# A hybrid Fourier / attention / DeltaNet block: the context triangular systems spread over all partitions, eight interleaved rows of a system in each

## The chip, the cores and the metric

The kernel runs on one core of a Trainium2 chip. The metric is the time of one execution on the device in microseconds (us); a version is judged by the median of its runs. Engines are named as in the profile: PE (TensorE matmul), PEld (TensorE weight load), DVE (VectorE), ACT (ScalarE), POOL (GpSimd) and SP (SyncE, which here only issues DMAs; its queue is SPq in the profile).

## The reference

One layer mixes 1024 latent tokens (width 1024) and 256 context tokens. One input projection feeds three groups of heads: a Fourier group, attention (8 query heads, 2 key/value heads) and a gated DeltaNet with 4 heads of 64. Then come an output projection and a squared-ReLU MLP. Cut to the DeltaNet, whose triangular systems the change touches:

```
z = h @ lp['w_in']                       # f, aq, ak, av, dqkv, dz, gates
dqkv = silu(dwconv(dqkv, conv_w))        # q, k, v of the DeltaNet
lmat = where(strict, einsum('nbhid,nbhjd->nbhij', kb, kc) * decay, 0.0)
tmat = triangular_solve(eye + lmat, eye, left_side=True, lower=True)
u = einsum('nbhij,nbhjd->nbhid', tmat, vb)
w = einsum('nbhij,nbhjd->nbhid', tmat, kb * exp(gc)[..., None])
# per chunk n: S -> S', o   (a sequential scan over the chunks)
o_f, s_f = chunk_gdn(forward);  o_b, s_b = chunk_gdn(reversed)
```

Each chunk of each head and of each direction has a unit triangular matrix that has to be inverted. The scan over the context gives the states from which the scan over the latents starts, so context and latents both need their inverses (tmat).

## The kernel before, in words

The kernel uses chunks of CK = 32 tokens: NCL = 32 latent chunks and NCC = 8 context chunks. With 4 heads and 2 directions d that makes 256 latent systems and 64 context systems, each 32x32. All products are emulated in three matmuls from a high and a low half (L236, L237, L238: high by high, high by low, low by high), so each weight is split: ACT writes the high half (helper L220) and DVE subtracts it (L448) for the low half. L238 is the matmul that needs the low half.

The stage in question lies about 200 to 320 us after the start. In it PE runs, one after the other, the second half of the query projection, the DeltaNet's v columns (`w_dv`), its q columns (`w_dq`), and the columns `w_dz` and `w_f` for the gate and the Fourier group, between them short groups of matmuls that regroup v by chunk (`compact`, L629) and at the end the transposes of the keys (`k_T`), with which attention begins. `conv_proj` clears the padding of the convolution's input with three memsets on POOL (L579 to L581), projects on PE and copies with ACT; `conv_silu` convolves and applies SiLU on DVE (L596, L597, L598, L603, L605). The regrouping L629 of the second v half waits for L603.

Beside that run the triangular systems. `grams()` forms the matrices L on PE, masks them on DVE (L739) and stores them to a DRAM scratch `lsc[d]` (L740). `solve(d, lat, eng)` (L747 to L764) then inverts: direction 0 on DVE, direction 1 on POOL, each first for the context and then for the latents. One system lies in one partition as a 32x32 matrix U: the 32 context systems of a direction take 32 partitions (in the half of `KQT` that q takes later, tile z2a in the profile), the 128 latent systems all 128 (in `trib[d]`, tile fbase). Four DMAs load (L754), a POOL memset puts ones on the diagonal (L755), 30 steps of two instructions each (L760 multiplies a column by a row into `tmps[d]`, L761 adds) do the elimination in place, and four DMAs store to the scratch `tsc[d]` (L764). L895 and L897 load the inverses, of the context and of the latents, into `TT`, which the scan reads.

The two solves are generators that `tick()` advances while PE instructions are being written (`systems()` for direction 0, `system1()` for direction 1); after w_dq they are forced on until both context solves are written, and at the end drained. A scheduler then fixes the order of instructions on each engine while the kernel is built. An engine works strictly in that order, and so does SP: what stands behind a waiting instruction waits too. PE's order and ACT's order are the same in both kernels.

Of the kernel before, what the change touches and what calls it, by code (L numbers as in the profile page):

```python
# [14 lines left out]
ALU = mybir.AluOpType  # L15
AX = mybir.AxisListType

P = 128
# [9 lines left out]
CK = 32  # L28
VC_ = 68
NCL = S // CK  # L30
NCC = CTX // CK
# [143 lines left out]
def view(b, off, *shape):  # L175
    v = Buf.__new__(Buf)
    v.arena, v.shape, v.at = b.arena, (P,) + shape, b.at + off
    v.n = int(np.prod(shape))
    return v
# [12 lines left out]
def body(tc, t, out):  # L192
# [3 lines left out]
    with ctx:  # L196
# [14 lines left out]
        V, G, T, Y, SC = nc.vector, nc.gpsimd, nc.tensor, nc.sync, nc.scalar  # L211

        def buf(*shape, top=False, a=None, at=None):
            return Buf(a or Fa, (P,) + shape, top, at)
# [338 lines left out]
        for p, xs in enumerate((xs1, xs2, xs3, xs4)):  # L553
            norm_in(xs)
            g, c0 = ((0, 256), (1, 0), (1, 256), (2, 0))[p]
# [18 lines left out]
        KQT, KTC, KC, VC = kqt(), ktc(), kc(), vc()  # L574
        zrb, yb, thb = buf(S + 2 + CTX + 2), buf(S + CTX), buf(S + CTX)
        trib = [buf(S) for _ in range(2)]
# [112 lines left out]
        for d in range(2):  # L689
            R = view(vc, 0, NCA, CK)() if d else FF_[1]  # L690
            mk = C[("mle", "mge")[d]]
            G.tensor_tensor(R, GTT[:, 2 + d, :].unsqueeze(2).to_broadcast([P, NCA, CK]), mk.unsqueeze(1).to_broadcast([P, NCA, CK]), op=ALU.mult)
            for c in range(0, NCA, 16):
                n = min(16, NCA - c)
# [25 lines left out]
        lsc = [dram.tile([P, NCA, CK], F32, name=f"lsc{d}") for d in range(2)]  # L720
        tsc = [dram.tile([P, NCA, CK], F32, name=f"tsc{d}") for d in range(2)]
# [5 lines left out]
        def grams():  # L727
            for c in list(range(NCL, NCA, 8)) + list(range(0, NCL, 8)):
                b = gb.next()
                bv = b[:, 0 : 8 * CK].rearrange("p (c w) -> p c w", w=CK)  # L730
                for q in range(8):
                    for h in range(4):
                        hp, h2 = h // 2, h % 2
                        r = slice(64 * h2, 64 * h2 + 64)
                        k_ = KQT[r, hp, 0, (c + q) * CK : (c + q + 1) * CK] if c < NCL else KTC[r, hp, (c + q - NCL) * CK : (c + q - NCL + 1) * CK]
                        pe(T.matmul(bv[32 * h : 32 * h + 32, q, :], k_, k_, start=True, stop=True))
                for d in range(2):
                    l_ = lst.next()()
                    V.scalar_tensor_tensor(l_, bv, -1.0, FF_[d][:, c : c + 8, :], op0=ALU.mult, op1=ALU.mult)  # L739
                    Y.dma_start(lsc[d][:, c : c + 8], l_)  # L740
                yield
                yield
            done.append(1)

        tmps = [buf(256) for _ in range(2)]

        def solve(d, lat, eng):  # L747
            c0, n = (0, NCL) if lat else (NCL, NCC)
            nu = 4 * n
            pr_ = slice(0, nu) if lat else slice(nu * d, nu * d + nu)  # L750
            flat = trib[d]()[pr_] if lat else KQT[pr_, 0, 1, :]
            U = flat.rearrange("p (m i) -> p m i", i=CK)
            for h in range(4):
                Y.dma_start(U[h * n : (h + 1) * n], lsc[d][32 * h : 32 * h + 32, c0 : c0 + n, :].rearrange("j c i -> c j i"))  # L754
            G.memset(flat[:, 0 : S : CK + 1], 1.0)  # L755
            for s in range(1, CK - 1):
                j, ms, is_ = (s, slice(0, s), slice(s + 1, CK)) if d == 0 else (CK - 1 - s, slice(CK - s, CK), slice(0, CK - 1 - s))
                nm, ni = s, CK - 1 - s
                tv = tmps[d]()[pr_, 0 : nm * ni].rearrange("p (m i) -> p m i", i=ni)
                eng.tensor_tensor(tv, U[:, ms, j : j + 1].to_broadcast([nu, nm, ni]), U[:, j : j + 1, is_].to_broadcast([nu, nm, ni]), op=ALU.mult)  # L760
                eng.tensor_tensor(U[:, ms, is_], U[:, ms, is_], tv, op=ALU.add)  # L761
                yield
            for h in range(4):
                Y.dma_start(tsc[d][32 * h : 32 * h + 32, c0 : c0 + n, :].rearrange("j c i -> c j i"), U[h * n : (h + 1) * n])  # L764

        def systems():
            for _ in range(GRAM):
                yield
            yield from grams()
            yield from solve(0, False, V)  # L770
            solved.append(1)
            yield from solve(0, True, V)

        def system1():
            while not done:
                yield
            yield from solve(1, False, G)
            solved.append(1)
            yield from solve(1, True, G)


        def q_sink(half):
# [10 lines left out]
        for half in range(2):  # L793
            w_q = wgroup([(COL_AQ + half * 256, 256)])
            if half:
                tasks += [[systems(), 2, 3], [system1(), 2, 3]]
                pinned = True
            proj_N(w_q, 256, range(NT), q_sink(half))
# [584 lines left out]
        for n in range(NPR * 5):  # L1383
            j, k = n // 5, n % 5
# [8 lines left out]
            h = j // 4  # L1393
# [114 lines left out]
        for n4 in range(4):  # L1508
# [9 lines left out]
            for q in range(NT):  # L1518
                b = omr.next()[:, 0:256]
                for k in (0, 1, 2, 3, 4, 6, 7, 5):  # L1520
                    h, l = halves[k // 4]
# [221 lines left out]
        for pn, (prods, blocks) in enumerate(PASSES):  # L1743
            for pc in range(NPC):
                U, W = {}, {}
# [3 lines left out]
                for w in blocks:  # L1749
                    W[w] = raww.next()()  # L1750
                    j, k = int(w[0]) - 1, int(w[1]) - 1
# [11 lines left out]
                for n in prods:  # L1763
                    if n in WSUM:
                        x, y, op = WSUM[n]
# [38 lines left out]
```

## Time and profile before

| | us |
|---|---|
| time, median of 3 runs (lowest to highest) | 1457.31 (1456.09 to 1457.76) |
| time of the profiled execution | 1456.26 |
| span of the profiled execution (first to last instruction) | 1454.5 |
| busy: PE / DVE / ACT / POOL | 1384.1 / 1005.7 / 703.6 / 668.5 |
| context solve on DVE, first to last instruction | 201.87 to 261.85 |
| latent solve on DVE | 261.89 to 313.81 |
| context solve on POOL | 207.24 to 267.00 |
| latent solve on POOL | 267.24 to 320.42 |

A row of a timeline gives the start in us from the beginning of the span, the duration in us, engine, line and operation, the tile written and the tiles read, their partitions x elements, and in brackets how long the engine had been idle before it and what released it. Short neighbouring instructions on DVE overlap by some 0.1 us in their records. The clock column (PEclk) of a table of windows is the TensorE clock that was granted, as a share of full speed.

### The profile page before, as it was taken

What the parts mean: (1) busy time and instruction counts of PE and PEld (TensorE: products, weight loads), DVE (VectorE), ACT (ScalarE), POOL (GpSimd) and SP (SyncE); (2) the same over time, 40 slices, a digit from 0 to 9 for tenths busy, and PEclk for the clock granted to TensorE, in tenths of its full rate; (3) what the DMA queues carried; (4) which work ended last, traced back from release to release, by engine and by line L of the source; (5) the groups of instructions that cost most, each with busy time, mean ns of one, the idle gap of its engine ahead of it and who ended that gap; (6) DMA issues with size and microseconds to landing.
All of it is one profiled execution on the core that took longest, in us unless ns stands there. A gap on an engine that the chain in (4) does not pass through costs nothing.

```text
span 1454.5 us, 28942 instructions
## 1 busy us (share of the span) xinstructions
PE 1384.1 (95%) x11462; PEld 1117.6 (77%) x11462; DVE 1005.7 (69%) x1695; ACT 703.6 (48%) x1239; POOL 668.5 (46%) x739
## 2 busy tenths in 40 slices
PE   4899988989999999989899899999999999999997
PEld 1677977766777777778799777888888888888886
DVE  0774679986878877786633887655556576776984
ACT  1742422323777777776412654554545443443331
POOL 2653679973446466374433733444443100010782
PEclk8999999999999999999999999999999999999999
DMA  8973141242000010042322315544446898766641
GB/s 316 334 257 125 45 118 44 53 93 76 9 10 24 9 38 4 17 142 80 95 84 91 106 55 183 168 147 134 141 151 217 307 392 269 245 230 215 197 157 58
DMA packets 137304, 197.67 MB, mean 136 GB/s; under 512 B 45021, under 2 KB 80463, under 8 KB 136911
## 3 DMA queue, kind: packets, MB, share of 16 engines
q1 hardware_dynamic: 136464, 195.12, 41.0%
q8 instruction: 90, 1.47, 0.4%
q10 hardware_dynamic: 703, 0.69, 0.2%
q14 instruction: 47, 0.39, 0.1%
HBM read 149.84 MB, written 45.94 MB: 135 GB/s over the span
## 4 chain that ended last, share of the span: by engine, by line
PE 47%; DVE 2%; POOL 2%; DMA 1%; issue 1%; ACT 1%; SPq 0%; DVEq 0%; POOLq 0%; ACTq 0%
PE bk L237 8%; PE bk L238 8%; PE bk L236 8%; PE ba L236 7%; PE ba L237 7%; PE ba L238 7%; PE bk L233 1%; DVE z1b L1335 0%; PE ba L233 0%; DMA fbase<-w_out 0%; POOL rbase L1470 0%; DMA fbase<-la 0%; DMA la<-fbase 0%; DVE rbase L998 0%; POOL z2c L1734 0%
## 5 line engine op out<-in xcount | busy, mean ns | idle before, releaser
L220 ACT ACTIVATE rbase<-fbase 128x512 fp32r<-128x512 f32 (+3 forms) x255 | 171.4, 685 | 87.5 <-PE bk L237 54.8
L220 ACT ACTIVATE fbase<-bk 128x512 f32<-128x512 f32 (+3 forms) x224 | 124.9, 561 | 150.8 <-PE bk L233 81.0
L233 PE MATMUL bk<-rbase 128*128 128x256 f32 (+2 forms) x984 | 173.3, 311 | 4.4 <-ACT fbase L220 2.6
L233 PEld LDWEIGHTS bk<-rbase 128*128 128x128 f32 (+1 forms) x984 | 132.3, 175 | 34.1 <-ACT fbase L220 3.4
L220 ACT ACTIVATE z1c<-fbase 128x512 fp32r<-128x512 f32 (+1 forms) x120 | 76.8, 653 | 138.5 <-DMA fbase<-w_ff 51.8
L233 PE MATMUL ba<-rbase 128*65 128x512 f32 (+4 forms) x576 | 138.4, 343 | 5.6 <-DVE rbase L998 4.8
L1503 POOL TENSOR_TENSOR fbase<-fbase 128x512 f32<-128x512 f32 x64 | 87.4, 1366 | 114.4 <-DVE z1c L1470 81.2
L220 ACT ACTIVATE fbase<-fbase 128x512 f32<-128x512 f32 (+4 forms) x148 | 95.9, 659 | 90.6 <-POOL fbase L1626 27.2
L1708 POOL TENSOR_TENSOR z2c<-z2c,fbase 128x512 f32<-128x512 f32 x16 | 31.1, 1969 | 203.8 <-ACT z2c L220 127.9
L974 DVE TENSOR_REDUCE fbase<-ba 128x1 f32<-128x512 f32 (+1 forms) x192 | 106.4, 593 | 19.6 <-PE ba L233 18.3
L220 ACT ACTIVATE rbase<-z1d 128x1024 fp32r<-128x1024 f32 x61 | 63.0, 1055 | 101.9 <-PE bk L237 81.8
L1470 DVE TENSOR_TENSOR z1c<-fbase,z1c 128x512 fp32r<-128x512 f32 x112 | 91.5, 820 | 23.6 <-ACT z1c L220 19.7
L1470 DVE TENSOR_TENSOR rbase<-z1d,rbase 128x1024 fp32r<-128x1024 f32 x61 | 84.9, 1407 | 31.1 <-ACT rbase L220 30.9
L998 POOL TENSOR_TENSOR rbase<-fbase,rbase 128x512 fp32r<-128x512 f32 x56 | 72.1, 1287 | 67.2 <-ACT rbase L220 63.0
L236 PE MATMUL bk<-rbase 128*128 128x512 f32 x256 | 99.7, 389 | 0.0
L237 PE MATMUL bk<-rbase 128*128 128x512 f32 x256 | 99.7, 389 | 0.0
L238 PE MATMUL bk<-rbase 128*128 128x512 f32 x256 | 99.6, 389 | 0.0
L998 DVE TENSOR_TENSOR rbase<-fbase,rbase 128x512 fp32r<-128x512 f32 x104 | 80.5, 774 | 25.7 <-ACT rbase L220 25.3
L1470 DVE TENSOR_TENSOR rbase<-fbase,rbase 128x1024 fp32r<-128x1024 f32 (+1 forms) x65 | 81.0, 1265 | 21.8 <-ACT rbase L220 21.6
L233 PEld LDWEIGHTS ba<-rbase 128*65 128x65 f32 (+1 forms) x576 | 76.2, 155 | 23.3 <-DVE rbase L998 5.9
L238 PE MATMUL ba<-rbase 128*128 128x512 f32 x192 | 74.8, 389 | 0.0
L237 PE MATMUL ba<-rbase 128*128 128x512 f32 x192 | 74.7, 389 | 0.0
(349 smaller groups left out, 3815.8 us busy)
## 6 DMA issues: line engine op xcount, KB each, us to landing
fbase<-w_ff SPq DMA_DIRECT2D x70, 512.0 KB
u<-fbase SPq DMA_DIRECT2D x112, 256.0 KB
z2a<-w_mod SPq DMA_DIRECT2D x36, 512.0 KB
z1d<-w_ff SPq DMA_DIRECT2D x34, 512.0 KB
z1d<-u SPq DMA_DIRECT2D x33, 512.0 KB
fbase<-u SPq DMA_DIRECT2D x23, 512.0 KB
fbase<-w_in SPq DMA_DIRECT2D x16, 512.0 KB
fbase<-x SPq DMA_DIRECT2D x14, 512.0 KB
```

The costliest lines, as they stand in the source:

```text
L220: return SC.activation(o, i, f, **k)
L233: pe(T.matmul(o, l, r, start=start, stop=stop))
L236: pe(T.matmul(o, lh, rh, start=start, stop=False))
L237: pe(T.matmul(o, lh, rl, start=False, stop=False))
L238: pe(T.matmul(o, ll, rh, start=False, stop=stop))
L974: V.tensor_reduce(st4[:, z : z + 1], b, AX.X, ALU.max)
L998: (G if k2 in GP and not any(a <= n < b for a, b in NGP) else V).tensor_tensor(hl[:, :, 1], p, f32(hl[:, :, 0]), op=ALU.subtract)
L1470: eng.tensor_tensor(lo, i, f32(hi), op=ALU.subtract)
L1503: G.tensor_tensor(w[nm], w[a], w[b], op=op)
L1708: G.tensor_tensor(c, c, G2[cs_.start // 512], op=ALU.mult)
```

## The change

`solve` is split into `solve_ctx` and `solve_lat`. The latent part is the old code. In the context part a system takes four partitions instead of one. Partition group g (32 partitions, 8 for each head) holds of every system the rows g, g+4, ..., 8 rows of 32, as R in `KQT[:, 0, 1, d*256 : d*256+256]` (tile z2a), and a whole copy N of the matrix L in `trib[d]` (tile fbase). R begins as the identity (a memset to 0 and four memsets to 1 on POOL, L754 and L756 of the changed kernel), and 31 steps of two instructions (L762, L763) subtract multiples of its columns, each on 128 partitions; a step takes only the rows that can be other than zero.

```diff
-        def solve(d, lat, eng):
-            flat = trib[d]()[pr_] if lat else KQT[pr_, 0, 1, :]
...
+        def solve_ctx(d, eng):
+            N = trib[d](None, (P, CK, CK))
+            flat = KQT[:, 0, 1, d * 8 * CK : (d + 1) * 8 * CK]
+            R = flat.rearrange("p (m i) -> p m i", i=CK)
+            for g in range(4):
+                for h in range(4):
+                    Y.dma_start(N[32 * g + NCC * h : 32 * g + NCC * (h + 1)], lsc[d][32 * h : 32 * h + 32, NCL:, :].rearrange("j c i -> c j i"))
+            G.memset(flat, 0.0)
+            for g in range(4):
+                G.memset(flat[32 * g : 32 * g + 32, g : 8 * CK : CK + 4], 1.0)
+            for s in range(CK - 1):
+                j = s if d == 0 else CK - 1 - s
+                rs, is_ = (slice(0, j // 4 + 1), slice(j + 1, CK)) if d == 0 else (slice(j // 4, 8), slice(0, j))
+                nm, ni = rs.stop - rs.start, CK - 1 - s
+                tv = tmps[d]()[:, 0 : nm * ni].rearrange("p (m i) -> p m i", i=ni)
+                eng.tensor_tensor(tv, R[:, rs, j : j + 1].to_broadcast([P, nm, ni]), N[:, j : j + 1, is_].to_broadcast([P, nm, ni]), op=ALU.mult)
+                eng.tensor_tensor(R[:, rs, is_], R[:, rs, is_], tv, op=ALU.add)
+                yield
+            for g in range(4):
+                for h in range(4):
+                    Y.dma_start(tsc[d][32 * h + g : 32 * h + 32 : 4, NCL:, :].rearrange("r c i -> c r i"), R[32 * g + NCC * h : 32 * g + NCC * (h + 1)])
+
+        def solve_lat(d, eng):
+            nu = 4 * NCL
+            flat = trib[d]()
...
-            yield from solve(0, False, V)
+            yield from solve_ctx(0, V)
             solved.append(1)
-            yield from solve(0, True, V)
+            yield from solve_lat(0, V)
```

Summed over the steps, a context solve had 60 instructions of 30 to 240 elements, 4960 elements per partition in all for each of the two operations; it has 62 of 8 to 76 elements now, 1560. The loads of a direction are 16 DMAs of 8 partitions instead of 4, with four times the bytes; the stores 16 instead of 4 with the same bytes. Because N lies in `trib[d]`, the latent loads into the same buffer stand behind the context solve now. Numbers of lines behind L747 shift; those that are used below: L774 (latent loads), L775 (the latent diagonal's memset), L780 and L781 (latent steps), L767 (context stores), L753 (context loads); L816, the scaling of v on POOL, is L836.

How the scheduler orders this now is shown at three places. On DVE, around the low halves (L448) of `w_dq`; L922, L923 and L913 are small copies for the projection's rows. Before:

```order
L760 TENSOR_TENSOR fbase<-z2a 32x184
L761 TENSOR_TENSOR z2a<-z2a,fbase 32x23x8
L922 CAST rbase<-fbase 128x10
L760 TENSOR_TENSOR fbase<-z2a 32x168
L923 TENSOR_SCALAR rbase<-fbase 128x10
L448 TENSOR_TENSOR z1a<-fbase,z1a 128x1024
L761 TENSOR_TENSOR z2a<-z2a,fbase 32x24x7
L913 TENSOR_SCALAR rbase<-fbase 128x136
L448 TENSOR_TENSOR z1a<-fbase,z1a 128x1024
```

In the changed kernel, at the same place:

```order
L763 TENSOR_TENSOR z2a<-z2a,fbase 128x7x7
L762 TENSOR_TENSOR fbase<-z2a,fbase 128x42
L942 CAST rbase<-fbase 128x10
L943 TENSOR_SCALAR rbase<-fbase 128x10
L763 TENSOR_TENSOR z2a<-z2a,fbase 128x7x6
L448 TENSOR_TENSOR z1a<-fbase,z1a 128x1024
L762 TENSOR_TENSOR fbase<-z2a,fbase 128x35
L933 TENSOR_SCALAR rbase<-fbase 128x136
L448 TENSOR_TENSOR z1a<-fbase,z1a 128x1024
```

L448 still stands inside the context solve, behind 47 of 60 solve instructions before and 52 of 62 now, none of more than 76 elements.

On POOL, where the context solve ends and the latent one begins. Before:

```order
L760 TENSOR_TENSOR fbase<-z2a 32x58
L761 TENSOR_TENSOR z2a<-z2a,fbase 32x29x2
L760 TENSOR_TENSOR fbase<-z2a 32x30
L761 TENSOR_TENSOR z2a<-z2a,fbase 32x30
L580 MEMSET fbase 128x2
L760 TENSOR_TENSOR fbase<-fbase 128x30
L761 TENSOR_TENSOR fbase<-fbase 128x30
L581 MEMSET fbase 128x1
```

In the changed kernel:

```order
L762 TENSOR_TENSOR fbase<-z2a,fbase 128x8
L763 TENSOR_TENSOR z2a<-z2a,fbase 128x8
L580 MEMSET fbase 128x2
L581 MEMSET fbase 128x1 x2
L775 MEMSET fbase 128x32
L836 TENSOR_TENSOR z2a<-z2a,fbase 128x2560
L579 MEMSET fbase 128x1
L580 MEMSET fbase 128x2
L775 MEMSET fbase 128x32
L780 TENSOR_TENSOR fbase<-fbase 128x30
```

The diagonal of DVE's latent systems (the first L775) now stands behind POOL's whole context solve, and the large L836 ahead of POOL's latent solve instead of in its midst.

On SP, from the context loads to the context inverses; `lsc_1451` and `tsc_1453` are direction 0 (DVE), `lsc_1452` and `tsc_1454` direction 1 (POOL), `qd` holds the queries, and the L444 are the halves of weights: one of `w_dq`, two of `w_dz`, two of `w_f`. Before:

```order
L754 DMA fbase<-lsc_1451 32x32x32 x2
L444 DMA fbase<-w_in 128x4x256
L786 DMA qd<-z2a 128x256
L754 DMA fbase<-lsc_1451 32x32x32 x2
L754 DMA fbase<-lsc_1452 32x32x32 x4
L786 DMA qd<-z2a 128x256 x2
L444 DMA fbase<-w_in 128x4x256 x4
L764 DMA tsc_1454<-z2a 8x32x32 x2
L764 DMA tsc_1453<-z2a 8x32x32 x4
L764 DMA tsc_1454<-z2a 8x32x32 x2
L895 DMA fbase<-tsc_1453 128x256
```

In the changed kernel:

```order
L806 DMA qd<-z2a 128x256 x2
L753 DMA fbase<-lsc_1452 8x32x32 x10
L444 DMA fbase<-w_in 128x4x256 x3
L774 DMA fbase<-lsc_1451 32x32x32
L767 DMA tsc_1453<-z2a 8x8x32 x16
L774 DMA fbase<-lsc_1451 32x32x32 x3
L767 DMA tsc_1454<-z2a 8x8x32 x16
L774 DMA fbase<-lsc_1452 32x32x32 x4
L444 DMA fbase<-w_in 128x4x256 x2
L915 DMA fbase<-tsc_1453 128x256
```

The latent loads, all issued ahead of the weights before, stand behind the end of their direction's context solve and behind 16 and 32 stores; the two loads of `w_f` stand behind all of them.

More of the change, by code (lines that the diff above doesn't have):

```diff
@@ L745, in body @@
         tmps = [buf(256) for _ in range(2)]
-        def solve(d, lat, eng):
-            c0, n = (0, NCL) if lat else (NCL, NCC)
-            nu = 4 * n
-            pr_ = slice(0, nu) if lat else slice(nu * d, nu * d + nu)
-            flat = trib[d]()[pr_] if lat else KQT[pr_, 0, 1, :]
+        def solve_ctx(d, eng):
[22 more added lines that the diff above has]
+            flat = trib[d]()
             U = flat.rearrange("p (m i) -> p m i", i=CK)
             for h in range(4):
-                Y.dma_start(U[h * n : (h + 1) * n], lsc[d][32 * h : 32 * h + 32, c0 : c0 + n, :].rearrange("j c i -> c j i"))
+                Y.dma_start(U[h * NCL : (h + 1) * NCL], lsc[d][32 * h : 32 * h + 32, 0:NCL, :].rearrange("j c i -> c j i"))
             G.memset(flat[:, 0 : S : CK + 1], 1.0)
@@ L758, in solve @@
                 nm, ni = s, CK - 1 - s
-                tv = tmps[d]()[pr_, 0 : nm * ni].rearrange("p (m i) -> p m i", i=ni)
+                tv = tmps[d]()[:, 0 : nm * ni].rearrange("p (m i) -> p m i", i=ni)
                 eng.tensor_tensor(tv, U[:, ms, j : j + 1].to_broadcast([nu, nm, ni]), U[:, j : j + 1, is_].to_broadcast([nu, nm, ni]), op=ALU.mult)
@@ L763, in solve @@
             for h in range(4):
-                Y.dma_start(tsc[d][32 * h : 32 * h + 32, c0 : c0 + n, :].rearrange("j c i -> c j i"), U[h * n : (h + 1) * n])
+                Y.dma_start(tsc[d][32 * h : 32 * h + 32, 0:NCL, :].rearrange("j c i -> c j i"), U[h * NCL : (h + 1) * NCL])
         def systems():
@@ L776, in system1 @@
                 yield
-            yield from solve(1, False, G)
+            yield from solve_ctx(1, G)
             solved.append(1)
-            yield from solve(1, True, G)
+            yield from solve_lat(1, G)
         def q_sink(half):
```

## The prediction

> **What bounds the kernel now.** I read the page's first lines, then the waits of PE between 180 and 420 us, then the timelines of the engines there. The page says that PE is the bound:
>
> ```profile
> span 1454.5 us, 28942 instructions
> PE 1384.1 (95%) x11462; PEld 1117.6 (77%) x11462; DVE 1005.7 (69%) x1695; ACT 703.6 (48%) x1239; POOL 668.5 (46%) x739
> ```
>
> So a faster solve is worth only the stalls of PE that it removes. This is all that PE waits for from the query projection to the first steps of the scan (who waited for whom: total us, times, longest):
>
> ```profile
> PE bk L238 <- DVE z1a L448: 9.9, 3, 6.0
> PE ba L238 <- DVE z1a L448: 3.5, 1, 3.5
> PE bk L629 <- DVE fbase L603: 2.3, 1, 2.3
> PE bk L736 <- DVE z2a L739: 2.2, 1, 2.2
> PE ba L233 <- DVE rbase L998: 0.7, 1, 0.7
> ```
>
> 18.6 us is the sum and no gain exceeds it by much. The stalls that touch the change are these three, with their place in time:
>
> ```profile
> 248.52 0.80 PE L238 MATMUL bk<-rbase,z1a 128*128 128x512 f32 x1 [6.04 <-DVE z1a L448]
> 252.10 0.63 PE L237 MATMUL bk<-rbase,z1a 128*128 128x512 f32 x1
> 264.53 6.29 PE L629 MATMUL bk<-fbase 64*32 64x64 f32 x160 [2.33 <-DVE fbase L603]
> 297.04 0.50 PE L238 MATMUL bk<-rbase,z1a 128*128 128x512 f32 x1 [3.17 <-DVE z1a L448]
> ```
>
> The first (w_dq) waits for a subtraction on DVE that stands in DVE's order behind most of the context solve; ACT had its input ready about 10 us earlier (235.53 + 2.01 = 237.5). The 0.63 row is one of 13 that ran slower after that stall than the usual 0.39 (page: 389 ns), and so costs some 13 x 0.19 = 2.5 us more. The third (w_f) waits for the same line inside the latent solve:
>
> ```profile
> 235.53 2.01 ACT L220 ACTIVATE z1a<-fbase 128x1024 fp32r<-128x1024 f32 x2 [0.53 <-PE ba L237]
> 247.26 1.21 DVE L448 TENSOR_TENSOR z1a<-fbase,z1a 128x1024 fp32r<-128x1024 f32 x1
> 295.31 1.67 DVE L448 TENSOR_TENSOR z1a<-fbase,z1a 128x1024 fp32r<-128x1024 f32 x1
> 318.67 0.68 DVE L941 CAST rbase<-bk 64x512 fp32r<-64x512 f32 x1 [1.65 <-ACT rbase L220]
> ```
>
> **The change, part by part.** *Steps on DVE.* Up to the subtraction for w_dq the old context solve has 47 instructions, 13.5 + 12.1 = 25.6 us (groups of DVE between 201.8 and 247.2), and single steps beside POOL and without it look like this:
>
> ```profile
> L760 DVE TENSOR_TENSOR fbase<-z2a 32x168 f32<-32x168 f32 (+14 forms) x24 | 13.5, 561 | 0.3
> L761 DVE TENSOR_TENSOR z2a<-z2a,fbase 32x184 f32<-32x184 f32 (+14 forms) x23 | 12.1, 528 | 0.4
> 265.34 0.39 DVE L761 TENSOR_TENSOR fbase<-fbase 128x84 f32<-128x84 f32 x1
> 312.56 0.25 DVE L761 TENSOR_TENSOR fbase<-fbase 128x84 f32<-128x84 f32 x1
> 318.63 0.36 POOL L761 TENSOR_TENSOR fbase<-fbase 128x84 f32<-128x84 f32 x1
> 319.82 0.25 POOL L760 TENSOR_TENSOR fbase<-fbase 128x30 f32<-128x30 f32 x1
> ```
>
> Now 52 instructions of at most 76 elements stand there. An 84-element one took 0.25 us with POOL waiting and 0.39 beside POOL, so the 52 cost 52 x 0.28 = 14.6 (with a gap of 0.03) to 52 x 0.39 = 20.3. The rest of DVE's work in that stretch (from 201.87 to 247.26 less 25.6, less 47 gaps of 0.04) is some 18 us, about 10 of it possible before the solve starts.
>
> *Loads.* The solve starts later: 16 DMAs instead of 4 for a direction. SP's issues there:
>
> ```profile
> 204.95 4.24 SPq L740 DMA_DIRECT2D lsc<-z2a  x4
> 212.04 5.75 SPq L754 DMA_DIRECT2D fbase<-lsc  x6
> 267.03 5.55 SPq L764 DMA_DIRECT2D tsc<-z2a  x8
> 248.50 10.30 SPq L444 DMA_DIRECT2D fbase<-w_in  x4
> ```
>
> A small DMA takes SP 5.55 / 8 = 0.69 us here, 0.96 for the larger load; the new small ones I put between 0.4 and 0.69. The last of them follow the last store of L (L740, 204.95 + 4.24 = 209.2) in part, so direction 0 lands at 214 to 217 instead of 202. Then the subtraction for w_dq ends at 214 + 8 + 14.6 + 1.2 = 237.8 at best and 217 + 8 + 20.3 + 1.2 = 246.5 at worst, about 242. PE arrives at 242.48 (248.52 less 6.04): 6.0 us of stall become 0 to 4, I take 0.5, and with them go the 2.5 us of slow matmuls. The load of w_dq's second half is moved behind all 32 context loads; there its cover is 10 us until ACT wants it.
>
> *The regrouping.* L629 waits for L603, which now follows the context solve instead of standing in the latent one:
>
> ```profile
> 263.26 1.21 DVE L603 SCALAR_TENSOR_TENSOR fbase<-fbase 128x1024 f32<-128x1024 f32 x1
> 270.39 0.75 DVE L596 TENSOR_SCALAR fbase<-fbase 128x1024 f32<-128x1024 f32 x1 [1.42 <-PE bk L629]
> ```
>
> I get it done near 256 instead of 264.5, so PE is 8 us ahead at that point.
>
> *The handover to the latent solve, on which the rest hangs.* Before it needed nothing: the loads were there. Now three things end before DVE's first latent step (call it T). DVE's own context end: near 247, then some 9 us of convolution. SP: one latent load, 16 stores, three loads, then 3 us to land: 246.3 + 16 x (0.4 to 0.69) + 3 x 0.5 + 3 = 257 to 262. POOL: the memset of the diagonal stands behind POOL's whole context solve. In POOL's order a memset (L579) stands ahead of it that waits for DVE's L597:
>
> ```profile
> 226.65 1.27 DVE L597 SCALAR_TENSOR_TENSOR fbase<-fbase 128x1024 f32<-128x1024 f32 x1
> ```
>
> With less solve ahead that row comes some 4 us earlier, so POOL starts near 223.5. It has 62 steps of about 0.37 (0.25 to 0.36 each by the rows above, and 0.08 between), 23 us; to this come the blockings by DVE's large instructions, as now:
>
> ```profile
> 253.64 6.46 POOL L761 TENSOR_TENSOR z2a<-z2a,fbase 32x168 f32<-32x168 f32 x1
> 279.34 4.63 POOL L816 TENSOR_TENSOR z2a<-z2a,fbase 128x2560 f32<-128x2560 f32 x1
> 280.14 4.08 DVE L760 TENSOR_TENSOR fbase<-fbase 128x228 f32<-128x228 f32 x1
> 261.89 0.31 DVE L760 TENSOR_TENSOR fbase<-fbase 128x30 f32<-128x30 f32 x1
> ```
>
> Some 15 us of those (6.5 at the convolution, 3.4 at L448, and the rest in waits at the start) give 262. So T is 262, between 257 and 270, against 261.89 before: the whole gain of the context solve is spent on waiting for loads and for POOL.
>
> *Inside the latent solve* L603 with its small neighbour (1.7 us) and the idle 1.42 are gone, 3.1 us. The subtraction for w_f stood 35.1 us after the start (297.0 with its end); five steps (3.7) fewer are ahead of it now, so it ends at T + 28.2; the latent solve ends at T + 48.8, 313.81 before. The keys' transposes follow, where DVE had 1.65 us of idle and about 0.7 more to spare. PE's lead is thus at most 297.04 - 28.2 - T = 268.8 - T at w_f and 313.81 + 2.3 - 48.8 - T = 267.3 - T at the keys. For T = 262 that is 5.3; I take 4.8, for a rest of the w_f stall.
>
> *Things moved at no cost.* The w_f loads, now behind 32 stores and the latent loads, are issued near 271 and land near 275. ACT splits them when PE has let go of the buffer:
>
> ```profile
> 284.81 1.06 ACT L220 ACTIVATE z1a<-fbase 128x1024 fp32r<-128x1024 f32 x1 [1.97 <-PE ba L237]
> ```
>
> With a lead of 8.6 us that is 276; PE wants the high half just before the w_f stall (297.04 - 3.17 = 293.9, less the lead 285). Some 9 us of cover, if it goes each us more is a us of PE. POOL's latent solve starts near 270, since its loads follow the last stores, and ends 5 to 12 us after the old end of 320.4. Its inverses have a long cover: the scan runs the context first,
>
> ```profile
> 355.57 0.43 PE L233 MATMUL bk<-z1b,z2a 64*32 64x64 f32 x16
> 361.11 0.43 PE L233 MATMUL bk<-z1b,z2a 64*32 64x64 f32 x16
> 327.86 0.82 SPq L897 DMA_DIRECT2D fbase<-tsc  x2
> ```
>
> 8 steps 5.5 us apart, so latent inverses are wanted near 400, not at 328. The zero and identity memsets stand near 75 us on POOL, well ahead.
>
> *The sum*: w_dq's stall gains 5.5 and the slow matmuls 2.5, the regrouping's 0.6 more; of these 8.6 us the handover lets 4.8 through. Against the profiled execution: 1456.26 - 4.8 = 1451.5. The median of the runs shown, 1457.31, is 1.05 higher; by it the time is 1452.5.
>
> A row that bears on POOL: 280.14 shows DVE held for 4.08 us while L816 ran. The Trainium skill, "SBUF — State Buffer", section "Who interferes with whom", says more: a DVE instruction with two SBUF inputs and a GpSimd instruction that reads SBUF exclude each other for the whole instruction. By that rule all pairs of steps would run one after the other, and the sum would be a loss of some 4 us (the fourth case below). The row 265.34, with 0.39 for DVE while POOL stepped too, speaks against so strict a form for short instructions.
>
> The Trainium skill, "DMA: Bandwidth & Descriptors", section "Rules for kernel authors", advises to coalesce small transfers, since under 64 KB one pays mostly overhead. Taken as a serial 2 us for each of the 16 (an estimate), it would put T at 285 and the time above 1470; eight stores in 5.55 us show that issues overlap the flights, so I give it no chance of its own.
>
> **The rivals.**
>
> *A, as above*, T between 260 and 264: a gain of 3 to 7, 1450 to 1454.
>
> *B, handover early.* POOL is blocked less, since a short step leaves DVE's instructions more gaps, and the stores issue at 0.4: T = 257, the lead 267.3 - 257 = 10.3, the time 1447; at most all of PE's three stalls and the slow matmuls, 1445.5. For it: 6.46 us is one instruction's wait, not a rate. Against: the convolution's five large instructions stand back to back in the new order.
>
> *C, nothing comes through.* POOL's context solve starts or ends 5 us later, or SP is as slow as 0.69 for each store and 0.96 for each load: T = 266 to 268, lead 0 to 1. The time is 1455 to 1459. For it: both chains come out within 5 us of the old start.
>
> *D, slower.* DVE and POOL steps exclude each other: a pair costs 0.25 + 0.37 = 0.62 instead of 0.39, and with some 40 pairs that is 9 us, on DVE's path as on POOL's. T becomes 271, the lead 267.3 - 271 = -3.7, the time 1461; 1465 if the stores issue at 0.69 besides (T = 275). It decides from T = 270.2 on (267.3 + 2.9). For it: the row of 4.08. Against: 0.39.
>
> That the spread solve is no shorter than the old one is a rival I exclude: 1560 elements instead of 4960, and 62 instructions at 0.39 are 24 us against 30 x (0.56 + 0.53) = 33 before.
>
> **How the numbers follow.** A 0.40, B 0.18, C 0.23, D 0.19. What a measurement can tell from no change is about 0.2%, 2.9 us. Faster by more: A and B, 0.58; within: C, 0.23; slower: D, 0.19. The likeliest time is A's 1452.5, its own range 1450 to 1454. The range for 8 in 10 takes B down to its bound, 1445.5, and of D the lower half, 1460.5.
>
> **What would show it.** Right: PE's wait at w_dq falls from 6.0 to under 4 us; the first latent step on DVE stays near 262, with idle ahead of it that ends with POOL's memset (L775) or a load; the wait at L629 shrinks; the one for w_f stays at 1 to 3 us. Wrong: an idle DVE until 270 or later, a wait of ACT for w_f's load, a DVE step of 0.6 us in the context solve, or the latent inverses on the chain that ends last.

## The result, and the profile after

The changed kernel takes 1445.95 us (median; 1444.78 to 1448.01) where the kernel before took 1457.09 in the same comparison: a ratio of 0.9929, with a 95% interval of 0.9917 to 0.9940. That is 11 us less. The profiled execution has a span of 1443.0 us against 1454.5.

What PE waits for between 180 and 420 us, in the view that the prediction quotes of before (total us, times, longest):

```profile
PE bk L616 <- ACT fbase L220: 2.6, 1, 2.6
PE bk L736 <- DVE z2a L739: 2.4, 1, 2.4
PE ba L238 <- DVE z1a L448: 1.3, 1, 1.3
PE bk L629 <- DVE fbase L603: 0.8, 1, 0.8
PE ba L233 <- DVE rbase L1018: 0.7, 1, 0.7
```

The three waits of 9.9 us on low halves (w_dq and w_f) are gone altogether, those of w_dv and of the regrouping are down from 3.5 to 1.3 and from 2.3 to 0.8, and there is one that was not there before: L616, 2.6 us (the group of small matmuls that sums the squares of q for its normalisation; its input comes from ACT, and ACT's from L603 on DVE). The sum fell from 18.6 to 7.8 us. PE's timeline at those places, in order of time:

```profile
240.11 0.39 PE L238 MATMUL bk<-rbase,z1a 128*128 128x512 f32 x1
251.77 4.66 PE L629 MATMUL bk<-fbase 64*32 64x64 f32 x160 [0.77 <-DVE fbase L603]
303.24 0.67 PE L616 MATMUL bk<-fbase 64*32 64x2 f32 x32 [2.64 <-ACT fbase L220]
304.35 0.63 PE L237 MATMUL bk<-rbase,z1a 128*128 128x512 f32 x1
316.95 0.94 PE L233 MATMUL ba<-rbase 128*128 128x512 f32 x2
```

Since PE's order is the same in both, the start of one matmul in both traces gives PE's lead. It is 237.13 - 234.91 = 2.2 us ahead of w_dq (from w_dv), 248.52 - 240.11 = 8.4 at w_dq, 264.53 - 251.77 = 12.8 at the regrouping, and 18.8 behind w_f (304.76 - 285.98, the first L616 of both). Then it falls: 319.32 (in the timeline of before, the L616 that waits now) - 303.24 = 16.1, and 327.69 - 316.95 = 10.7 for the L233 behind it. From there it stays at about 11 to the end. So of nearly 19 us won, 8 were given back at one place, 2.6 by the wait and the rest by a slow stretch behind it, which the table of windows shows (us, PE, PEld, DVE, ACT, POOL busy with counts, granted clock, DMA share, GB/s):

```profile
290.00:300.00 10.00, 10.00 (x106) 7.78 (x105) 9.31 (x21) 3.56 (x9) 7.43 (x14) 1.00 0.46 116
304.00:316.00 12.00, 12.00 (x135) 8.10 (x136) 5.41 (x10) 4.24 (x10) 8.39 (x18) 0.50 0.87 188
319.00:323.00 4.00, 4.00 (x62) 2.82 (x61) 2.34 (x6) 1.27 (x2) 0.68 (x1) 1.00 0.64 240
```

For 12 us PE was busy at a granted clock of 0.50, with 0.63 us for a matmul that takes 0.39 elsewhere: from 303.24 to 316.95 it needed 13.7 us for what took 8.4 before.

The engines around it, DVE, POOL and SP, at the handover from the context solve to the latent one:

```profile
241.51 0.18 DVE L763 TENSOR_TENSOR z2a<-z2a,fbase 128x8 f32<-128x8 f32 x1
250.44 1.27 DVE L603 SCALAR_TENSOR_TENSOR fbase<-fbase 128x1024 f32<-128x1024 f32 x1 [1.34 <-ACT fbase L220]
252.03 0.21 DVE L780 TENSOR_TENSOR fbase<-fbase 128x30 f32<-128x30 f32 x1
254.63 0.15 POOL L775 MEMSET fbase<- 128x32 f32 x1
257.14 5.36 POOL L836 TENSOR_TENSOR z2a<-z2a,fbase 128x2560 f32<-128x2560 f32 x1 [2.36 <-ACT z2a L220]
258.07 4.61 DVE L780 TENSOR_TENSOR fbase<-fbase 128x150 f32<-128x150 f32 x1
241.92 6.07 SPq L767 DMA_DIRECT2D tsc<-z2a  x16
248.04 1.71 SPq L774 DMA_DIRECT2D fbase<-lsc  x3
```

DVE's latent solve begins at 252.03, 9.9 us earlier than before, and ahead of the memset of the diagonal (254.63) that the prediction let it wait for. Sixteen stores took SP 6.07 us, 0.38 each.

### The profile page after: what moved, and what is told of

It reads as the page before. It is cut to its first block, busy times and chain, and to the rows that moved or that the text cites. A ratio compares the mean times of both kernels' runs of the same rounds, so it can differ in the third digit from the quotient of the medians.

```text
span 1443.0 us, 28992 instructions
## 1 busy us (share of the span) xinstructions
PE 1384.1 (96%) x11462; PEld 1116.0 (77%) x11462; DVE 987.1 (68%) x1697; ACT 703.4 (49%) x1239; POOL 645.7 (45%) x749
## 4 chain that ended last, share of the span: by engine, by line
PE 48%; DVE 3%; DMA 2%; POOL 2%; issue 1%; ACT 0%; SPq 0%; DVEq 0%; POOLq 0%; ACTq 0%
PE bk L237 8%; PE bk L238 8%; PE bk L236 8%; PE ba L236 7%; PE ba L237 7%; PE ba L238 7%; PE bk L233 1%; DMA fbase<-la 1%; DMA la<-fbase 0%; DVE z1b L1355 0%; DMA fbase<-w_out 0%; POOL rbase L1490 0%; DMA fbase<-x 0%; PE bk L241 0%; DVE rbase L1018 0%
## 5 line engine op out<-in xcount | busy, mean ns | idle before, releaser
L233 PE MATMUL bk<-rbase 128*128 128x256 f32 (+2 forms) x984 | 172.9, 310 | 4.4 <-ACT fbase L220 2.5
L233 PEld LDWEIGHTS bk<-rbase 128*128 128x128 f32 (+1 forms) x984 | 131.7, 174 | 34.1 <-ACT fbase L220 3.3
L233 PE MATMUL ba<-rbase 128*65 128x512 f32 (+4 forms) x576 | 138.2, 342 | 5.6 <-DVE rbase L1018 4.3
L233 PEld LDWEIGHTS ba<-rbase 128*65 128x65 f32 (+1 forms) x576 | 76.1, 154 | 23.6 <-DVE rbase L1018 5.4
```

The lines of the kernel that those rows point to most:

```text
L233: pe(T.matmul(o, l, r, start=start, stop=stop))
```

## The experiments

**What sets the pace of a step.** In the changed kernel DVE and POOL step side by side between 229 and 236 us. In the traces of before and after (DVE, POOL; each in order):

```profile
240.17 0.72 DVE L761 TENSOR_TENSOR z2a<-z2a,fbase 32x228 f32<-32x228 f32 x1
240.93 0.68 DVE L760 TENSOR_TENSOR fbase<-z2a 32x220 f32<-32x220 f32 x1
240.73 0.65 POOL L760 TENSOR_TENSOR fbase<-z2a 32x238 f32<-32x238 f32 x1
241.45 0.67 POOL L761 TENSOR_TENSOR z2a<-z2a,fbase 32x238 f32<-32x238 f32 x1
```

```profile
231.22 0.34 DVE L762 TENSOR_TENSOR fbase<-z2a,fbase 128x60 f32<-128x60 f32 x1
231.60 0.36 DVE L763 TENSOR_TENSOR z2a<-z2a,fbase 128x60 f32<-128x60 f32 x1
231.18 0.30 POOL L762 TENSOR_TENSOR fbase<-z2a,fbase 128x66 f32<-128x66 f32 x1
231.56 0.32 POOL L763 TENSOR_TENSOR z2a<-z2a,fbase 128x66 f32<-128x66 f32 x1
```

On both engines the starts are about equally far apart: 0.76 and 0.72 before, 0.38 and 0.38 after. From 229.0 to 235.9 both start 19 instructions of the solve: one of DVE passes for one of POOL. Which of the two sets the time can be seen when only one of them gets long instructions. Both kernels are the changed one with one engine's `rs`, the rows that a step takes, widened to all eight:

```diff
-                rs, is_ = (slice(0, j // 4 + 1), slice(j + 1, CK)) if d == 0 else (slice(j // 4, 8), slice(0, j))
+                rs, is_ = (slice(0, j // 4 + 1), slice(j + 1, CK)) if d == 0 else (slice(0, 8), slice(0, j))   # POOL long
+                rs, is_ = (slice(0, 8), slice(j + 1, CK)) if d == 0 else (slice(j // 4, 8), slice(0, j))       # DVE long
```

> POOL's context steps take all 8 rows (up to 248 elements, 3968 in all instead of 1560); DVE's are those of the changed kernel. Theory (lock step): while both engines step, one DVE instruction takes as long as one POOL instruction; DVE's steps of 48 to 76 elements go from 0.39 us apart to 0.6 to 0.7, the subtraction for w_dq comes at 243 to 248, PE waits there 4 to 7 us, and the time is 1451 to 1458 us. Rival (DVE's own size sets its pace): DVE's steps stay at 0.39 and the time at 1444 to 1449 us.

> The mirror image: DVE's context steps take all 8 rows (up to 248 elements), POOL's are those of the changed kernel. Theory (lock step): DVE's steps are not more than 0.45 us apart although they have three times the elements, and PE waits at w_dq for under 3 us: 1444 to 1450 us. Rival (own size): 0.65 to 0.75 us apart, a wait of 5 us or more at w_dq, 1452 to 1458 us.

With POOL's long, DVE's unchanged steps slow down to POOL's pace, PE waits 5.4 us at w_dq, and the time is 1454.05 us (0.9978 of before, 0.9968 to 0.9988):

```profile
232.15 0.60 DVE L763 TENSOR_TENSOR z2a<-z2a,fbase 128x64 f32<-128x64 f32 x1
232.78 0.65 DVE L762 TENSOR_TENSOR fbase<-z2a,fbase 128x75 f32<-128x75 f32 x1
232.11 0.56 POOL L762 TENSOR_TENSOR fbase<-z2a,fbase 128x208 f32<-128x208 f32 x1
232.74 0.60 POOL L763 TENSOR_TENSOR z2a<-z2a,fbase 128x208 f32<-128x208 f32 x1
245.53 0.79 PE L238 MATMUL bk<-rbase,z1a 128*128 128x512 f32 x1 [5.37 <-DVE z1a L448]
```

In the changed kernel, where DVE is idle (302.03 to 303.70), POOL's steps of 198 elements are 0.64 us apart too (302.57 and 303.21), so this pace is POOL's own. With DVE's long, 160 elements instead of 60 cost it next to nothing, and PE does not wait for w_dq:

```profile
231.07 0.33 DVE L762 TENSOR_TENSOR fbase<-z2a,fbase 128x160 f32<-128x160 f32 x1
231.43 0.33 DVE L763 TENSOR_TENSOR z2a<-z2a,fbase 128x160 f32<-128x160 f32 x1
231.26 0.27 POOL L762 TENSOR_TENSOR fbase<-z2a,fbase 128x48 f32<-128x48 f32 x1
231.61 0.29 POOL L763 TENSOR_TENSOR z2a<-z2a,fbase 128x48 f32<-128x48 f32 x1
273.47 0.19 DVE L780 TENSOR_TENSOR fbase<-fbase 128x30 f32<-128x30 f32 x1 [3.42 <-DMA fbase<-lsc]
```

The rows at 231 us alone do not show a lock step, since 168 elements cost DVE by itself 0.37 us as well (264.13 to 264.50 in the changed kernel, where POOL waits). Those at 235 us do: DVE's steps of 120 and 112 elements are 0.40 apart (235.17 and 235.57), as POOL's of 76 are (235.07 and 235.47), where 108 elements cost DVE by itself 0.30 (275.30 to 275.60, with POOL waiting). So the lock step holds, and POOL, slower for each element, sets the pace. The time of this kernel was forecast wrongly, though: 1467.83 us (1.0067; 1.0046 to 1.0088). With the longer steps the scheduler put 15 of POOL's stores ahead of DVE's latent loads on SP, and the last row shows what came of it: the latent solve at 273.5, behind a DMA. PE then waited 6.6 us at L616 and 10.4 for a load of queries.

**One direction alone.** The old `solve` is kept for the other direction; R lies in the second half of `KQT`, which that one does not use.

```diff
-            yield from solve_ctx(1, G)
+            yield from solve(1, False, G)      # DVE alone is spread
-            yield from solve_ctx(0, V)
+            yield from solve(0, False, V)      # POOL alone is spread
```

> Only direction 0 (DVE) has the spread context solve, direction 1 (POOL) the old one. Theory: the gain is DVE's. Its queue reaches the subtraction for w_dq before PE needs it, so PE's wait there stays under 2 us, and the first latent step on DVE comes near 254: 1446 to 1450 us. Rival (the prediction's handover): DVE's latent solve waits for POOL's memset of the diagonal behind POOL's context solve, which ends near 267 as before, so the lead is lost: 1455 to 1458 us.

> Only direction 1 (POOL) has the spread context solve, direction 0 (DVE) the old one. Theory: the 47 old instructions still stand ahead of the subtraction for w_dq on DVE, only somewhat shorter beside a lighter POOL; PE waits there 3 to 6 us and the first latent step on DVE comes at 256 to 262: 1451 to 1457 us. Rival (POOL's part carries the gain, through the handover or the port): 1446 to 1450 us.

DVE alone: 1460.85 us (1.0027; 1.0012 to 1.0042), outside both expectations. POOL's old instructions of 220 to 240 elements hold DVE's short ones to some 0.7 us each, and PE waits 7.5 us at w_dq, more than before. That alone does not make it slower than before: at L616 PE still started 2.6 us earlier (316.70 against 319.32). Behind it come a wait of 2.62 us that the profile puts down to a DMA and 10 us at a granted clock of 0.50 (322 to 332), which the expectation did not have. POOL alone: 1456.46 us (1.0000; 0.9991 to 1.0010), in the range, but not by the way forecast. At w_dq PE waited only 1.5 us and led by 12.6 at the regrouping; then a single wait took it all:

```profile
236.90 0.40 SPq L444 DMA_DIRECT2D fbase<-w_in  x1
253.89 0.30 SPq L774 DMA_DIRECT2D fbase<-lsc  x1
254.29 5.72 SPq L767 DMA_DIRECT2D tsc<-z2a  x16
263.79 1.21 SPq L444 DMA_DIRECT2D fbase<-w_in  x2
268.35 1.06 ACT L220 ACTIVATE z1a<-fbase 128x1024 fp32r<-128x1024 f32 x1 [14.75 <-DMA fbase<-w_in]
270.08 3.63 PE L629 MATMUL bk<-fbase 64*32 64x64 f32 x64 [15.33 <-ACT z2a L220]
```

The second half of w_dz (263.79) stood on SP behind a latent load and 16 stores, which wait for POOL's context end; ACT waited for that weight, and the copy for PE stood behind it. To separate this from the solve itself, R got a buffer of its own and N the second half of `KQT`, so that no latent load waits for a context solve:

```diff
-            N = trib[d](None, (P, CK, CK))
-            flat = KQT[:, 1, 1, d * 8 * CK : (d + 1) * 8 * CK]
+            N = KQT[:, 1, 1, :].rearrange("p (m i) -> p m i", i=CK)
+            flat = rown()
```

> Direction 1 (POOL) alone is spread, as in the run with POOL alone before, but its R and N lie in buffers of their own, so that no latent load on SP stands behind a context solve and none ahead of the weights. Theory: POOL's short instructions are what DVE's old, long steps needed; PE waits under 2 us at w_dq, and the lead that the former run lost behind SP is kept: 1438 to 1447 us. Rival (DVE's half is needed as well): 1450 us or more.

> Direction 0 (DVE) alone is spread, with R and N in buffers of their own, so that no latent load stands behind a context solve. Theory: POOL's old instructions of up to 240 elements still set DVE's pace (0.65 to 0.7 us a step); PE waits 5 to 8 us at w_dq: 1450 to 1460 us. Rival (the run with DVE alone was slow only by the order on SP): under 1447 us.

DVE alone stays at 1455.50 us (0.9987; 0.9974 to 1.0000) with a wait of 9.3 us at w_dq, longer even than forecast: its half gains nothing clear of the noise on its own, in either order on SP. POOL alone missed again, 1456.65 us (0.9995; 0.9982 to 1.0009): the latent loads were out of the way, the 16 stores were not, and PE waited 12.3 us for the same copy. So POOL was made to issue those stores itself:

```diff
-                    Y.dma_start(tsc[d][32 * h + g : 32 * h + 32 : 4, NCL:, :] ...
+                    (G if d else Y).dma_start(tsc[d][32 * h + g : 32 * h + 32 : 4, NCL:, :] ...
```

> As the run before with POOL alone spread and buffers of its own, but POOL issues the 16 stores of its context inverses itself, so that nothing on SP stands between the two halves of w_dz. Theory: the lead of 12 us that POOL's short instructions gave by 252 us, and that the two former runs lost to a late w_dz, is kept in large part: 1441 to 1449 us. Rival (DVE's own half is needed for the rest): the next wait takes it, 1451 us or more.

1448.73 us (0.9946; 0.9928 to 0.9963). POOL's half alone gains 7.9 us, against 11.1 for the whole change, when SP does not take it back (the whole change was not run with these stores on POOL). PE led by 14 to 16 us from the regrouping on, and waited 9.4 at w_f, where both engines stood in their latent solves.

**The handover.** Two kernels test what DVE's latent solve waits for. In one the multiplication of every POOL context step is issued twice; in the other direction 0's N lies in `KQT`'s second half.

```diff
                 eng.tensor_tensor(tv, R[:, rs, j : j + 1]...
+                if d == 1:
+                    eng.tensor_tensor(tv, R[:, rs, j : j + 1]...
```

```diff
-            N = trib[d](None, (P, CK, CK))
+            N = trib[d](None, (P, CK, CK)) if d else KQT[:, 1, 1, :].rearrange("p (m i) -> p m i", i=CK)
```

> Each multiplication of POOL's context solve is issued twice: 31 more instructions of the same size, so that POOL's solve ends some 12 us later, near 266, and with it the memset that stands behind it. Theory: DVE's latent solve does not wait for that memset; its first step stays at 251 to 255 us and the time at 1444 to 1450 us. Rival (the handover of the prediction): the first step comes at 266 or later, PE's lead is lost: 1455 to 1460 us.

> Direction 0's copy N lies in another buffer, so its latent loads are issued before its context solve ends, as in the old kernel. Theory: the first latent step on DVE waited for DVE's own convolution, not for the loads: it stays at 251 to 253 and the time at 1444 to 1448 us. Rival (the prediction's: stores and loads on SP set the handover): the step comes 3 us or more earlier and the time is 1440 to 1443 us.

With POOL's solve longer, the memset came at 267.11 and DVE's first latent step at 253.37, so DVE does not wait for it:

```profile
253.37 0.29 DVE L782 TENSOR_TENSOR fbase<-fbase 128x30 f32<-128x30 f32 x1
267.11 0.15 POOL L777 MEMSET fbase<- 128x32 f32 x1
281.27 0.39 DVE L783 TENSOR_TENSOR fbase<-fbase 128x228 f32<-128x228 f32 x1
304.67 0.37 SPq L953 DMA_DIRECT2D fbase<-kvd  x1
311.12 1.01 SPq L973 DMA_DIRECT2D fbase<-qd  x2
314.77 1.03 PE L241 MATMUL bk<-fbase 128*64 128x128 f32 x4 [9.74 <-DMA fbase<-qd]
```

The time, 1453.03 us (0.9979; 0.9968 to 0.9990), is that of neither theory. POOL's latent solve ended later (328.4), with it the split of v that stands in POOL's order, so a load of keys and values waited 15.4 us on SP and the queries behind it came late: PE waited 9.7 us. The third row, from a stretch in which POOL only waits, shows what 228 elements cost DVE by itself: 0.39, against 0.69 to 0.72 beside POOL in the trace of before.

With N elsewhere, the kernel takes 1440.75 us (0.9887; 0.9867 to 0.9907), some 5 us less than the changed one. Here my theory fell and its rival held: the loads on SP do set the handover, not by a wait in the trace but, as it seems, by the order of instructions that the scheduler makes from them. It now starts the latent solve at 242.3 instead of behind the convolution, and the wait at L616 is gone.

**The place that gave 8 us back.** L616 waits for ACT, ACT for L603 on DVE, and L603 stands behind the latent solve. One instruction of that solve was held for 4.61 us (258.07, above) while POOL scaled v (L836). In this kernel the scaling follows POOL's latent solve, by a factor that also reads the solve's last rows, times zero:

```diff
-        G.tensor_tensor(VC, VC, NK[:, 0].unsqueeze(2)...
...
         tasks.clear()
+        late = tmps[1]()[:, 0:NCA]
+        G.tensor_scalar(late, trib[1]()[:, 30 * CK : 30 * CK + NCA], 0.0, None, op0=ALU.mult)
+        G.tensor_tensor(late, late, NK[:, 0], op=ALU.add)
+        G.tensor_tensor(VC, VC, late.unsqueeze(2)...
```

> The scaling of v on POOL (the 5 us instruction that blocked DVE for 4.6 us in the latent solve) is made to follow POOL's latent solve. Theory: DVE's latent solve ends 4 us earlier (295), L603 behind it ends by 299, PE's wait of 2.6 us at L616 vanishes and with it the 13 us at half clock behind it (5.5 us lost): 1437 to 1440 us. Rival 1: the half clock there comes from the small matmuls and not from the wait, so only 2.6 us are gained: 1443 to 1444 us. Rival 2: the later scaling holds up the scan: 1446 us or more.

> Direction 0's copy N in its own buffer and the late scaling together. Theory: each alone takes away the same thing, PE's wait at L616 with the half clock behind it, so together they bring little more: 1436 to 1440 us. Rival: they act at different places and their gains of 5 and 7 us add up: 1432 to 1435 us.

1438.81 us (0.9882; 0.9853 to 0.9910): 7 us less than the changed kernel, as expected, for a wait of 2.6. There is no wait at L616, and the granted clock from 304 to 316 is 1.00:

```profile
298.82 1.28 DVE L603 SCALAR_TENSOR_TENSOR z2a<-fbase 128x1024 f32<-128x1024 f32 x1
304.00:316.00 12.00, 11.11 (x201) 7.69 (x197) 6.58 (x13) 4.01 (x9) 10.65 (x18) 1.00 0.74 155
```

L603 came only 2 us earlier, at 298.82 instead of 300.77 (not the 4 forecast), which was enough. Both edits together give 1438.34 us (0.9873; 0.9857 to 0.9888): each removes the wait at L616, and they don't add up. This is the fastest version found, though not to be told from the one before it, some 18 us under the kernel before.

## Why the prediction was right, and where it was not

The direction and the range held; the likeliest value, 1452.5, was 6.5 us too high, and the gain of 4.8 less than half of what came. What happened is nearest to the prediction's second case (an early handover, 1447 us).

*The lower end of the range* held by luck. 1445.5 was meant as the most that the change could bring, all three stalls and the slow matmuls, and the time came 0.45 us above it. The rows that the prediction shows give 6.0 + 2.3 + 3.2 + 2.5 = 14.0 us for these, not the 11.8 by which 1445.5 lies under 1457.3, since the regrouping was counted with 0.6 and w_dq with 5.5. And PE won 18.8: the 2.2 us from w_dv, the slow part of the regrouping (6.29 us before, 4.66 now) and a second wait at w_f (0.73) were put at nothing. That the time is not lower is due to L616, which the prediction did not have; the three kernels without that wait took 1438.3 to 1440.8.

*w_dq.* Right: the first subtraction ended at 237.75 on DVE, at the best bound (237.8), and the 6.0 us of stall and the slow matmuls went. The 52 instructions ahead of it took 14.8 us, 0.28 each; beside POOL they were 0.38 apart. The 0.39 was taken as what an instruction costs beside POOL, whatever POOL runs. It is POOL's own pace, as the widened rows showed, so the number was right for a reason that I had not seen.

*The handover, T = 262.* This is the step that failed: T was 252.03. Three of its terms were wrong. POOL's memset was taken for a gate, and it isn't one: it came at 254.63, behind DVE's first steps, and it writes the diagonal, which those steps neither read nor write. POOL's blockings were carried over as 15 us from two long rows; POOL's whole context solve took 222.93 to 254.35, 31.4 us instead of 38. The stores took 0.38 us each, below the range of 0.4 to 0.69, and DVE's context solve ended at 241.7 instead of 246.3. What stood ahead of the first step, in the scheduler's order, was DVE's own convolution; the idle time that was named as the sign of a right prediction was not there.

*The regrouping and w_f.* The regrouping was put at 256 and came at 251.77. A rest of 1 to 3 us at w_f was expected; none was left.

*The limit behind it.* That the latent solve's end would bound PE's lead was right in kind, and so was its size: with T = 252.03 the prediction's 267.3 - T is 15.3, and 16.1 was left. The place was L616 and not the transposes of the keys, the limit there 16 us and not 5.3, and that a wait of 2.6 would cost 8 was not forecast at all.

*Things moved at no cost.* The w_f loads were issued at 263 and hidden, as said. POOL's latent solve ended at 311.6, before and not after the old end, so its cover was not tried here; the run with POOL's steps doubled shows that it is thin. Only the use of the inverses was counted there; the split of v and the loads queued on SP, which come first, were left out.

*The fourth case*, steps that exclude each other, was priced at 0.62 a pair. A pair took 0.38, as long as POOL's instruction with its gap. The Trainium skill, "SBUF — State Buffer", section "Who interferes with whom", has the loser of the port that VectorE and GpSimd share wait for the whole instruction. The trace agrees in that DVE's 75 elements took 0.65 us beside POOL's 0.60 in the run with long rows, and 150 elements 4.61 us beside L836. What the prediction drew from it, that the two times add up, is what the rows don't show.

## What to carry to other kernels

Where two engines run short element-wise instructions side by side, look at the distance of their starts: if it is equal on both, as here, the slower engine's instructions may set it, and that is the engine whose instructions to shorten; here, shortening the other's alone gained nothing. Before spreading work out, write down what each queue issues behind the new end: four of these eleven runs lost PE's lead, or most of it, to a load that stood late on SP, which the count of instructions does not show. And when a stall is removed, follow the lead to the next place that takes it back; here it was worth more than half as much as the change itself.

## What the runs showed of the hardware

The clock: a wait of 2.64 us at L616 was followed by 12 us at a granted clock of 0.50, though PE was busy all that time; the wait of 3.17 us at w_f before (297.04) was not:

```profile
294.00:297.00 3.00, 0.00 (x0) 0.00 (x0) 2.97 (x4) 0.04 (x1) 2.77 (x4) 1.00 0.00 0
297.00:300.00 3.00, 2.96 (x12) 2.18 (x12) 2.93 (x4) 0.00 (x0) 2.69 (x5) 1.00 0.00 0
```

In the kernel with POOL's long rows, a wait of only 1.61 us at the same L616 was followed by 12 us at 0.50 as well:

```profile
312.00:324.00 12.00, 11.89 (x135) 8.25 (x136) 4.30 (x8) 3.62 (x8) 10.34 (x22) 0.50 0.58 132
```

The 6.04 us at w_dq before were followed by 6 (248 to 254). So the length of a wait alone does not tell. Behind L616 PE runs groups of 32 matmuls of two columns between the large ones, behind w_dq only large ones. Without a wait the same groups ran at 1.00 (before, 318 to 332), so they do not lower the clock by themselves; whether they keep it down once it is low, or where the wait falls does, was not tried and stays open. The Trainium skill, "TensorE: Matmul & The Clock Gate", Part 1, has the clock fall to half after at least one idle window of about 3.4 us. The 6.04 us at w_dq agree with that; the waits of 1.61 and 2.64 us do not, since they are shorter and the clock fell.
